# Expert weights in 4 KB rows: two experts a tile, two tiles a step, a longer ring, and an earlier overflow branch

## The chip, the cores and the metric

The kernel runs on one core of one Trainium2 chip. Its time is what the device needs for one execution, in microseconds (us). Of three runs of the kernel before, the median is 1256.03 us (1255.78 to 1259.5). The profile is of one further execution.

## What is computed

256 tokens of width 1024 go through two transformer blocks, all in float32. The first block ends in a mixture of experts: each token is sent to two of 32 experts, and every expert's weights are read, used or not. The part that matters here:

```
def hier_moe(v, w_grp, b_grp, w_exp, b_exp, w_gate, w_up, w_down):
    ...                                   # group and expert of each token, weight of each
    for e in range(MOE_N_EXPERTS):        # 32
        hdn = jax.nn.silu(vt @ w_gate[e]) * (vt @ w_up[e])          # 1024 -> 512, twice
        y = y + (combine[:, e:e + 1].astype(hdn.dtype) * hdn) @ w_down[e]   # 512 -> 1024
    return y.reshape(bsz, seq, d).astype(v.dtype)
```

Each expert has three matrices of 2 MB (512 x 1024 float32), so the experts' weights are 192 MB in all, counted in units of 1,048,576 bytes. The second block works on the same 256 tokens and on 256 context tokens. The context tokens' half does not depend on the first block.

## The kernel before

The program has four stages: the first block's mixer, the experts (`experts`), and the two layers of the second block (`x0`, `x1`). While the experts run, a second stream (`side`: `ctx0`, then `ctx1`) does the context tokens' half of the second block. `drive` takes instructions from the streams by planned costs (`yield`), and so fixes the order of TensorE (PE) when the program is built. What is planned to take how long (`DMA_TILE` for one tile's load, `DMA_MB` for a side tile's) decides how much side work stands between two products of the experts.

The experts are taken four at a time, in eight groups `q`. For each expert up to 32 tokens are collected (`slots`: a product with a selection matrix `SY` makes `xg`, the collected tokens with the model dimension on the partitions, in eight blocks of 128). The four experts of a group stand side by side in 32 columns of the array each, so four products of 128x32 by 128x512 run together.

A weight tile holds 1 MB: 128 rows of one matrix of all four experts, in 512 columns, so 4 x 2 KB on each partition. A group has 24: eight of `w_gate`, eight of `w_up`, eight of `w_down` (four row blocks for each half of the 1024 columns), 192 in all. Tiles 1 to 9 of the stage are read ahead, five into memory that is used later (`early`: kB, kB, vB, kA, kTc) and four into the ring `we` of `WE` = 4 buffers. From then on a tile's load waits until PE has done with the tile four before it. All of these loads are issued by SyncE (SP), in program order; an instruction of SP that waits holds back all loads behind it.

The side stream has its own weight tiles (`wst`), three buffers of the pool `ws`. Most are 1024 rows by 256 columns, so 8 x 1 KB on each partition. `side_next` asks for the next tile when it hands out the last one that is loaded.

If an expert is chosen by more than 32 tokens, the tokens above 32 go through a slow loop (`overflow`). `fullest` counts, every engine then reads the count (`TENSOR_LOAD` on PE, SP and the others) and branches. With these inputs the branch isn't taken. It stands at the start of group 1; SP's `TENSOR_LOAD` there waits for all DMA counters, and so for every load that was issued.

`h` is the residual stream. `hs` is a copy of it, made by GpSimd (POOL), from which the slots of groups 1 to 7 are collected, while `h` is added to.

Of the kernel before, what the change touches and what calls it, by code (L numbers as in the profile page):

```python
# [8 lines left out]
F32 = mybir.dt.float32  # L9
# [9 lines left out]
D = 1024  # L19
KD = 8  # L20
NEG = -1e30
EPS = 1e-6
CH = 2304
# [9 lines left out]
DMA_LAT = 1000  # L33
DMA_TILE = 2580
DMA_MB = 2600
AHEAD_S = 1
# [141 lines left out]
class Feed:  # L178
# [92 lines left out]
class Net:  # L271
# [94 lines left out]
    def ws_tile(self):  # L366
        return self.ws.tile([128, CH], F32, name="wst", tag="wst", bufs=WS)

# [665 lines left out]
    def mixer_out(self):  # L1034
# [7 lines left out]
        self.pre.append(next(self.tiles))  # L1042
        self.load_ctx(self.vc)
        wr = self.t(A, [128, KD, 36], "gqk")
        nc.gpsimd.dma_start(wr[:, :, 0:4], I["w_grp"][0].rearrange("(k p) n -> p k n", p=128))
# [81 lines left out]
    def route(self):  # L1127
# [72 lines left out]
    def overflow(self):  # L1200
# [3 lines left out]
        with tc.If(most > 32):  # L1204
            co = self.t(self.B, [128, 2, 32], "over")
            self.ts(co, self.rk, 32.5, op0=OP.is_ge)
            self.tt(co, co, self.C.rearrange("p t g e -> p t (g e)"), OP.mult)
            vT, w, hT = self.kTc, self.vc.rearrange("p t (a n) -> p (t a) n", a=2), self.row.rearrange("p (k n) -> p k n", k=4)
            for i in range(2):
                self.ts(self.vc[:, i], self.hs[:, i], self.y0[:, i:i + 1])  # L1210
            g = self.vcol("g_ffn", 0, 8)
            for k2 in range(4):
                b = self.transposes([(256 * j + 128 * i, self.vc[:, i, (2 * k2 + j) * 128:(2 * k2 + j + 1) * 128])
                                     for j in range(2) for i in range(2)], self.pt, "t", 2)
                self.tt(vT[:, 2 * k2:2 * k2 + 2], b.rearrange("p (k t) -> p k t", k=2),
                        g[:, 2 * k2:2 * k2 + 2, None].to_broadcast([128, 2, 256]), OP.mult)
            sc = self.dram.tile([32, 128, 2], F32, name="cover")
            for i in range(2):
                nc.sync.dma_start(sc.rearrange("e p t -> p t e")[:, i], co[:, i])
            with tc.For_i(0, 32, 1) as e:  # L1220
                cw = self.t(self.B, [128, 2], "cwe")
                nc.sync.dma_start(cw, sc[bass.ds(e, 1)].rearrange("a p t -> p (a t)"))

                def load(ap):
                    nc.sync.dma_start(w, ap.rearrange("a (k p) n -> p (a k) n", p=128))
                    return w
                gu = []
                for n, tag in (("w_gate", "g"), ("w_up", "d")):
                    bs = [self.bank(self.pe, tag, 2) for _ in range(2)]
                    for hf in range(2):  # L1230
                        v = load(I[n][0][bass.ds(e, 1), 512 * hf:512 * hf + 512])
# [12 lines left out]
                for hf in range(2):  # L1244
                    v = load(I["w_down"][0][bass.ds(e, 1), :, 512 * hf:512 * hf + 512])
                    for i in range(2):
# [4 lines left out]
                        self.stt(o, b, cw[:, i:i + 1], o, OP.mult, OP.add)  # L1251

    def slots(self, q):

# [15 lines left out]
        self.slot[q] = xg, (ST, w)  # L1270
        g = self.vcol("g_ffn", 0, 8)
        src = self.hs if q else self.h
        for k4 in range(2):
            b = self.bank(pt, "t", 2)
            for k in range(4):
                for i in range(2):
                    kk = 4 * k4 + k
                    nc.tensor.matmul(b[:, 128 * k:128 * k + 128], src[:, i, 128 * kk:128 * kk + 128], Sy[:, i],
                                     start=i == 0, stop=i == 1)
# [12 lines left out]

    def early(self):

        P = self.Q0
        b = self.t(self.Qa, [128, 2, 2048], "kB")
        yield b[:, 0]
        yield b[:, 1]
        yield self.t(P, [128, 2048], "vB")
        yield self.t(self.Qa, [128, 2048], "kA")  # L1300
        yield self.t(self.P2, [128, 2048], "kTc")

    def expert_tiles(self):

        I, early = self.I, self.early()
        for q in range(8):
            es = slice(4 * q, 4 * q + 4)
            aps = [I[n][0][es, 128 * k:128 * k + 128, :] for n in ("w_gate", "w_up") for k in range(KD)]
            aps += [I["w_down"][0][es, 128 * k:128 * k + 128, 512 * hf:512 * hf + 512] for hf in range(2) for k in range(4)]
            if not q:  # L1310
                aps = aps[WE:WE + EARLY] + aps[:WE] + aps[WE + EARLY:]
            for ap in aps:
                v = next(early, None)
                if v is None:
                    v = self.we.tile([128, 2048], F32, name="we", tag="we", bufs=WE)
                v = v.rearrange("p (e n) -> p e n", e=4)
                self.nc.sync.dma_start(v, ap.rearrange("e p n -> p e n"))
                yield v

    def expert_tile(self):  # L1320

        n = len(self.used)
        if n >= EARLY + WE:
            self.loaded = max(self.loaded, self.used[n - WE] + DMA_LAT) + DMA_TILE
# [3 lines left out]
        return v, late  # L1328

    def experts(self):  # L1330
# [4 lines left out]
        yield (-2, self.slots(0))  # L1335
        for q in range(8):
            if q == 1:
                self.overflow()
                self.gf = self.bcast_row(self.row, self.I["g_final"])
# [3 lines left out]
            for _ in range(2):  # L1343
                b = self.bank(self.pe, "g", 2)
                for k in range(KD):
                    if k == 4:
                        yield from self.wait("slot%d1" % q)
                    v, late = self.expert_tile()
# [5 lines left out]
                    if not q and WE + EARLY == KD * len(bs) + k + 1:  # L1354
                        self.keep()
                        self.done.add("keep")
                if not q and not bs:
                    self.fullest()
                    yield 400
# [14 lines left out]
            yield (450, 600)  # L1374
            ds = [self.bank(self.pe, "d", 2) for _ in range(2)]
            for hf in range(2):
                for k in range(4):
                    v, late = self.expert_tile()
# [418 lines left out]
    def ctx1(self):  # L1797
# [7 lines left out]
        for q in range(8):  # L1805
            wk = self.side_next()
            if q == 7:

                self.done.add("c6")
                yield from self.wait("experts")  # L1810
            b = self.bank(ps, "s", 2)
            if q < 4:
# [15 lines left out]
    def keep(self):  # L1828
# [7 lines left out]
        self.kA = self.t(self.Qa, [128, 4, 512], "kA", dt=F32R)  # L1836
        self.kTc = self.t(self.P2, [128, KD, 256], "kTc")
        self.gm = self.t(self.P2, [128, KD], "gm")
# [644 lines left out]
```

## Time and profile before

| | |
|---|---|
| median of three runs | 1256.03 us |
| the profiled execution | 1260.11 us |
| its span | 1258.0 us, 20010 instructions |
| PE busy | 1119.0 us, 89% |
| DVE, ACT, POOL busy | 564.2, 454.1, 191.8 us |
| read from HBM | 331.58 MB |

The span is cut into 40 slices of 31.45 us by the page. In slices 11 to 28 the DMA engines are over 90% busy and move 338 to 386 GB/s: that is the stage of the experts, from 291.04 us (the first product of an expert) to 879.28 us (the end of the last). Outside it they move 67 to 346 GB/s, and PE has most of its work in products of three parts (`gmm`).

How to read the rows further down. A windows row gives a stretch and its length, then the busy time (and count of instructions) of PE, PEld, DVE, ACT and POOL, PE's granted clock and the mean busy share of the DMA engines (both as a share of 1), and GB/s. A timeline row gives start, length, engine, line, operation, how many, and in brackets the idle time before it and what ended it. A busy PE is an engine that has a matmul in it, not one at its peak. PE's matmuls of float32 appear as two records for each product in the program. In the DMA view "GB/s" is given in 40 equal pieces of the window. Times "idle before" name what ended the idle time.

### The profile page before, as it was taken

The page shows a single profiled execution, that of the slowest core. Times are in us where ns is not written, and L with a number is a line of the kernel's source. Part 1 is how long each engine was busy: PE and PEld are TensorE (multiplying, and loading weights), DVE is VectorE, ACT ScalarE, POOL GpSimd, SP SyncE. Part 2 cuts the span into 40 slices and gives each one's busy share as a digit, 9 for nine tenths or more (in the row PEclk, how much of TensorE's full clock was granted, in tenths as well). Part 3 has the DMA queues.
Part 4 walks back from the last instruction along what each step waited for, and adds up shares of the span by engine and source line. Part 5 has one row for each costly group of instructions (what it writes and reads, how often), then busy time and mean ns, then how long its engine had stood idle before and what let it go on. Part 6 is the DMA issues. An engine that isn't in the chain of part 4 may idle for free. (4 is left out here: it accounts for less than half of the span.)

```text
span 1258.0 us, 20010 instructions
## 1 busy us (share of the span) xinstructions
PE 1119.0 (89%) x7855; PEld 778.4 (62%) x7855; DVE 564.2 (45%) x1401; ACT 454.1 (36%) x1109; POOL 191.8 (15%) x209
## 2 busy tenths in 40 slices
PE   5999999999879998788979899976999998899996
PEld 4878877785424553333336455521887787799996
DVE  5457664653121212432221211101788668777766
ACT  4534564541101101222220110101566653776663
POOL 6134012111000000000000000000311224325231
PEclk9999999988989999989999989977999999999999
DMA  7897579956999999999999999999445247365331
GB/s 252 283 305 251 189 208 323 346 187 237 363 338 375 378 379 382 386 373 357 363 354 378 382 379 378 376 386 362 135 133 157 67 107 169 118 163 130 101 119 67
DMA packets 228634, 337.63 MB, mean 268 GB/s; under 512 B 20021, under 2 KB 113274, under 8 KB 228538
## 3 DMA queue, kind: packets, MB, share of 16 engines
q1 hardware_dynamic: 227050, 333.78, 77.8%
q0 software_dynamic: 1072, 2.45, 0.8%
q8 instruction: 63, 1.03, 0.4%
q14 instruction: 33, 0.27, 0.1%
q10 hardware_dynamic: 416, 0.10, 0.1%
HBM read 331.58 MB, written 4.73 MB: 267 GB/s over the span
## 5 line engine op out<-in xcount | busy, mean ns | idle before, releaser
L318 ACT ACTIVATE whi<-wst 128x512 fp32r<-128x512 f32 (+4 forms) x240 | 149.1, 628 | 108.6 <-PE m L315 99.0
L1351 PE MATMUL g<-we,xg 128*32 128x512 f32 x984 | 145.6, 659 | 40.9 <-DMA we<-in_w_gate_dram 22.1
L218 DVE TENSOR_TENSOR wlo<-wst,whi 128x512 fp32r<-128x512 f32 (+4 forms) x180 | 138.2, 775 | 84.3 <-ACT whi L318 83.3
L218 POOL TENSOR_TENSOR wlo<-wst,whi 128x512 fp32r<-128x512 f32 (+4 forms) x60 | 80.5, 1343 | 495.9 <-ACT whi L318 420.8
L315 PE MATMUL m<-whi,uhi 128*128 128x256 f32 (+2 forms) x368 | 109.8, 298 | 2.6 <-ACT uhi L318 1.9
L315 PE MATMUL m<-wlo,uhi 128*128 128x256 f32 (+2 forms) x368 | 105.8, 288 | 2.7 <-POOL wlo L218 2.7
L315 PE MATMUL m<-whi,ulo 128*128 128x256 f32 (+2 forms) x368 | 105.7, 287 | 0.0
L315 PE MATMUL s<-cuT,wst 128*128 128x256 f32 (+1 forms) x368 | 90.6, 392 | 4.4 <-SPq L1204 4.4
L1381 PE MATMUL d<-we,hT 128*32 128x512 f32 x512 | 71.6, 639 | 25.3 <-DMA we<-in_w_down_dram 24.3
L315 PEld LDWEIGHTS s<-cuT,wst 128*128 128x128 f32 (+1 forms) x368 | 63.7, 183 | 44.8 <-issue 34.0
L1351 PEld LDWEIGHTS g<-we,xg 128*32 128x32 f32 x984 | 21.6, 112 | 100.4 <-DMA we<-in_w_up_dram 42.0
L315 PEld LDWEIGHTS m<-whi,uhi 128*128 128x128 f32 x368 | 71.4, 194 | 12.9 <-issue 5.8
L315 PE MATMUL m<-xhi,whi 128*128 128x256 f32 x256 | 75.6, 295 | 0.0
L315 PEld LDWEIGHTS m<-wlo,uhi 128*128 128x128 f32 x368 | 71.6, 194 | 2.9 <-POOL wlo L218 2.9
L315 PE MATMUL m<-xhi,wlo 128*128 128x256 f32 x256 | 72.3, 283 | 0.0
L315 PE MATMUL m<-xlo,whi 128*128 128x256 f32 x256 | 72.3, 282 | 0.0
L315 PEld LDWEIGHTS m<-whi,ulo 128*128 128x128 f32 x368 | 71.4, 194 | 0.3 <-POOL ulo L504 0.3
L315 PEld LDWEIGHTS s<-wst,cuT 128*128 128x128 f32 x256 | 43.7, 194 | 22.2 <-issue 17.6
L315 PE MATMUL s<-wst,cuT 128*128 128x256 f32 (+1 forms) x256 | 57.3, 369 | 0.0
L315 PEld LDWEIGHTS m<-xhi,whi 128*128 128x128 f32 x256 | 48.8, 191 | 2.7 <-issue 2.5
L315 PEld LDWEIGHTS m<-xlo,whi 128*128 128x128 f32 x256 | 48.9, 191 | 0.7 <-issue 0.5
L315 PEld LDWEIGHTS m<-xhi,wlo 128*128 128x128 f32 x256 | 48.8, 191 | 0.0
(592 smaller groups left out, 2183.2 us busy)
## 6 DMA issues: line engine op xcount, KB each, us to landing
we<-in_w_down_dram SPq DMA_DIRECT2D x64, 1024.0 KB
we<-in_w_up_dram SPq DMA_DIRECT2D x63, 1024.0 KB
we<-in_w_gate_dram SPq DMA_DIRECT2D x60, 1024.0 KB
we<-in_ada_w_dram SPq DMA_DIRECT2D x24, 1024.0 KB
wst<-in_c_in_w_dram SPq DMA_DIRECT2D x24, 1024.0 KB
wst<-in_w_in_dram SPq DMA_DIRECT2D x17, 1024.0 KB
wst<-in_ab_in_w_dram SPq DMA_DIRECT2D x16, 1024.0 KB
wst<-in_ab_out_w_dram SPq DMA_DIRECT2D x8, 1024.0 KB
```

Source lines behind the costliest of these rows:

```text
L218: (net.nc.gpsimd if pool else net.nc.vector).tensor_tensor(b, src, a, OP.subtract)
L315: mm(out, l, r, start=first and i == 0, stop=last and i == len(ps) - 1, skip_group_check=True)
L318: return self.nc.scalar.activation(out, in_, f, **kw)
L1351: nc.tensor.matmul(b[32 * e:32 * e + 32, :], xg[:, k, 32 * e:32 * e + 32], v[:, e], start=k == 0, stop=k == KD - 1)
L1381: nc.tensor.matmul(ds[hf][32 * e:32 * e + 32, :], hT[:, k, 32 * e:32 * e + 32], v[:, e], start=k == 0, stop=k == 3)
```

## The change

1. A tile now holds two experts instead of four, with rows of 4 KB. For `w_gate` and `w_up` a partition holds two consecutive rows of the matrix (rows 2p and 2p+1 of a block of 256: `(p r) n -> p (r n)`); for `w_down` it holds a whole row of 1024. Two tiles, one for each pair of experts, belong to a step (`expert_pair`), which makes eight products of each. Only the last group's `w_down` keeps the old tiles.
2. So that row pairs match, the collected tokens come in another order of the model dimension: `hs` is written in that order, group 0 reads `h` with a step of two elements (`pairs`), and `gp` holds `g_ffn` in that order (a small DMA of POOL).
3. The ring is four `we` buffers, one buffer `w3` taken from the three of the pool `ws`, and `kTc`; when the context tokens have been transposed out of `vc`, that joins it. `ctx1` takes `kTc` and `vc` out again. So six buffers, then seven, then six and five. Ten tiles are read ahead, in place of nine, and an eleventh goes into `vc` before the first product; of side tiles two are read ahead, in place of three.
4. `fullest` and `overflow` stand before the first product of group 0. The slow loop uses buffers of the side stream, and its loads read row pairs.
5. `DMA_TILE` goes from 2580 to 2500, `DMA_MB` from 2600 to 2700.

```
-DMA_TILE = 2580
-DMA_MB = 2600
+DMA_TILE = 2500
+DMA_MB = 2700
...
-            v = self.net.ws_tile()[:, :kd * n].rearrange("p (k n) -> p k n", k=kd)
+            v = (self.net.ws_tile() if self.loads % WS else self.net.w3_tile())[:, :kd * n].rearrange("p (k n) -> p k n", k=kd)
...
-        return self.ws.tile([128, CH], F32, name="wst", tag="wst", bufs=WS)
+        return self.ws.tile([128, CH], F32, name="wst", tag="wst", bufs=WS - 1)
+
+    def w3_tile(self):
+        return self.ws.tile([128, CH], F32, name="w3", tag="w3")
...
-        self.side_q = [next(self.sides) for _ in range(WS)]
-        self.pre += [next(self.tiles) for _ in range(EARLY + WE - 7)]
+        self.side_q = [next(self.sides) for _ in range(WS - 1)]
+        self.pre += [next(self.tiles) for _ in range(EARLY + WE - 6)]
...
-            nc.gpsimd.tensor_copy(self.hs[:, i], self.h[:, i])
+            nc.gpsimd.tensor_copy(self.hs[:, i].rearrange("p (j r c) -> p j r c", j=4, r=2), self.pairs(self.h[:, i]))
...
+    def pairs(self, row):
+
+        return row.rearrange("p (j c r) -> p j r c", j=4, r=2)
...
+            if not q and not k4:
+                self.fullest()
+                yield 400
...
-    def early(self):
+    def room(self):
 
         P = self.Q0
+        yield self.t(self.P2, [128, 2048], "kTc")
         b = self.t(self.Qa, [128, 2, 2048], "kB")
         yield b[:, 0]
         yield b[:, 1]
         yield self.t(P, [128, 2048], "vB")
         yield self.t(self.Qa, [128, 2048], "kA")
-        yield self.t(self.P2, [128, 2048], "kTc")
+        self.ring = ["we"] * WE + ["w3", "kTc"]
+        n = 0
+        while True:
+            if n == WE + 1:
+
+                self.ring.append(self.ring.pop(0))
+            n += 1
+            s = self.ring.pop(0)
+            self.ring.append(s)
+            if s == "we":
+                yield self.we.tile([128, 2048], F32, name="we", tag="we", bufs=WE)
+            elif s == "w3":
+                yield self.w3_tile()[:, :2048]
+            else:
+                yield self.t(self.P2, [128, 2048], s)
...
-            es = slice(4 * q, 4 * q + 4)
-            aps = [I[n][0][es, 128 * k:128 * k + 128, :] for n in ("w_gate", "w_up") for k in range(KD)]
-            aps += [I["w_down"][0][es, 128 * k:128 * k + 128, 512 * hf:512 * hf + 512] for hf in range(2) for k in range(4)]
+            es = [slice(4 * q + 2 * x, 4 * q + 2 * x + 2) for x in range(2)]
+            aps = [I[n][0][s, 256 * j:256 * j + 256, :].rearrange("e (p r) n -> p e (r n)", r=2)
+                   for n in ("w_gate", "w_up") for j in range(4) for s in es]
+            if q < 7:
+                aps += [I["w_down"][0][s, 128 * k:128 * k + 128, :].rearrange("e p n -> p e n") for k in range(4) for s in es]
...
+            if q == 0:
+                yield from self.wait("slot01")
+                self.overflow()
             if q == 1:
-                self.overflow()
                 self.gf = self.bcast_row(self.row, self.I["g_final"])
...
+                    v, late = self.expert_pair()
                     yield (0, late)
-                    for e in range(4):
-                        nc.tensor.matmul(b[32 * e:32 * e + 32, :], xg[:, k, 32 * e:32 * e + 32], v[:, e],
-                                         start=k == 0, stop=k == KD - 1)
-                    yield 1100
...
+                    for r in range(2):
+                        for e in range(4):
+                            nc.tensor.matmul(b[32 * e:32 * e + 32, :], xg[:, 2 * j + r, 32 * e:32 * e + 32],
+                                             v[e // 2][:, e % 2, 512 * r:512 * r + 512],
+                                             start=j == 0 and r == 0, stop=j == 3 and r == 1)
+                        yield 1000
...
+        self.ring.append("vc")
...
+            if q in (0, 4):
+                n = "vc" if q else "kTc"
+                self.ring.remove(n)
```

On PE the start of the stage reads as follows, first in the program before. `t<-SY,h` collects the tokens of group 0, `t<-M,tab` counts them (two rows of 128x32), `g<-...,xg` are the experts' products, `s<-wst,cuT` is side work.

```order
L315 MATMUL s<-wst,cuT 128x256 x2
L1278 MATMUL t<-SY,h 128x128 x8
L1351 MATMUL g<-we,xg 32x512 x4
L1278 MATMUL t<-SY,h 128x128 x8
L1351 MATMUL g<-we,xg 32x512 x4
L1286 MATMUL t<-tab,SW 128x128 x2
L1351 MATMUL g<-we,xg 32x512 x8
L1351 MATMUL g<-kB,xg 32x512 x8
```

There the first product stands behind the first half of the tokens alone, and the count comes later (it stands behind tile `kA`). The same place of PE in the changed program:

```order
L315 MATMUL s<-wst,cuT 128x256 x2
L1295 MATMUL t<-SY,h 128x128 x8
L315 MATMUL s<-wst,cuT 128x256 x2
L1201 MATMUL t<-M_3390,tab 128x32 x2
L1295 MATMUL t<-SY,h 128x128 x8
L1210 TENSOR_LOAD cnti
L1211 COMPARE_AND_BRANCH
```

Both halves of the tokens, the count and the branch now stand before the first product. (The rows between the branch and the first `g<-we,xg` are the slow loop, which is skipped.)

On SP, around the branch, the program before has these rows (`w_ukv` is a side tile's matrix).

```order
L1317 DMA we<-in_w_up_dram 128x4x512 x7
L1317 DMA we<-in_w_down_dram 128x4x512 x7
L371 DMA wst<-in_b_w_ukv_dram 128x2x1024
L1317 DMA we<-in_w_down_dram 128x4x512
L1203 TENSOR_LOAD cnti
L1203 ISA x2
L1317 DMA we<-in_w_gate_dram 128x4x512 x2
L1204 COMPARE_AND_BRANCH
```

The count is read behind all 24 tiles of group 0. In the changed program SP's branch stands here, behind the tiles that are read ahead:

```order
L374 DMA wst<-in_ab_in_w_dram 128x8x256
L1354 DMA we<-in_w_gate_dram 128x2x1024
L1354 DMA vc<-in_w_up_dram 128x2x1024
L1210 TENSOR_LOAD cnti
L1210 ISA x2
L1211 COMPARE_AND_BRANCH
```

So the branch has moved from the end of group 0's tiles to the end of the read-ahead, whose last tile now goes into `vc`.

In the dense part of the side stream (`ab_in` is the side tiles' matrix) SP reads as follows before, with the semaphores that a load waits for. `PE_49` is PE's counter, `DMAHW..` are counters of earlier loads.

```order
L1317 DMA we<-in_w_up_dram 128x4x512 [waits DMAHW6_49,PE_49]
L371 DMA wst<-in_ab_in_w_dram 128x8x256
L1317 DMA we<-in_w_up_dram 128x4x512 [waits DMAHW7_49,PE_49]
L1317 DMA we<-in_w_up_dram 128x4x512 [waits DMAHW0_49,PE_49]
L1317 DMA we<-in_w_up_dram 128x4x512 [waits DMAHW1_49,PE_49]
L371 DMA wst<-in_ab_in_w_dram 128x8x256
```

Each expert tile waits for PE here, the side tiles do not. And in the changed program (`w_4298` is a use of `w3`):

```order
L374 DMA wst<-in_ab_in_w_dram 128x8x256 [waits DMAHW4_49,PE_49]
L1354 DMA kTc<-in_w_down_dram 128x2x1024 [waits DMAHW5_49]
L1354 DMA we<-in_w_down_dram 128x2x1024 [waits DMAHW6_49]
L374 DMA wst<-in_ab_in_w_dram 128x8x256 [waits DMAHW7_49,PE_49]
L1354 DMA we<-in_w_down_dram 128x2x1024 [waits DMAHW0_49]
L1354 DMA we<-in_w_down_dram 128x2x1024 [waits DMAHW1_49]
L1354 DMA we<-in_w_gate_dram 128x2x1024 [waits DMAHW2_49]
L1354 DMA w_4298<-in_w_gate_dram 128x2x1024 [waits DMAHW3_49]
```

Now the side tiles carry the wait for PE: 18 of the 23 side loads of the changed program's stage wait for the last product of the side tile before the one that PE is at. The expert tiles behind such a load then often need no wait of their own. Where a side load waits, two expert tiles stand between it and the last one that PE has used in 11 cases, and four in 7.

## Rows read from the trace of the kernel before

**Rows 1.** Windows: the experts' stage; a light stretch; two stretches with much side work.

```profile
292.00:879.00 587.00, 503.17 (x2978) 244.38 (x2974) 119.45 (x276) 87.85 (x224) 6.17 (x6) 0.94 1.03 370
496.00:540.00 44.00, 32.45 (x242) 14.12 (x245) 17.94 (x54) 11.87 (x40) 0.00 (x0) 1.00 1.05 386
372.00:492.00 120.00, 112.33 (x664) 62.49 (x662) 21.00 (x37) 17.32 (x38) 1.05 (x2) 0.99 1.05 378
672.00:812.00 140.00, 129.82 (x728) 71.91 (x726) 25.36 (x56) 15.84 (x33) 0.00 (x0) 0.96 1.05 379
```

**Rows 2.** PE's waits, 292 to 879 us: line, releaser: us in total, times, longest.

```profile
PE d L1381 <- DMA we<-in_w_down_dram: 24.3, 25, 2.0
PE g L1351 <- DMA we<-in_w_gate_dram: 22.1, 19, 2.3
PE g L1351 <- DMA we<-in_w_up_dram: 18.0, 22, 1.6
```

**Rows 3.** Timeline of PE and ACT, end of the experts' stage.

```profile
844.11 1.94 PE L1351 MATMUL g<-we,xg 128*32 128x512 f32 x8 [0.78 <-DMA we<-in_w_up_dram]
...
849.52 1.94 PE L1351 MATMUL g<-we,xg 128*32 128x512 f32 x8 [0.78 <-DMA we<-in_w_up_dram]
...
877.34 1.94 PE L1381 MATMUL d<-we,hT 128*32 128x512 f32 x8 [1.67 <-DMA we<-in_w_down_dram]
...
880.99 0.69 ACT L318 ACTIVATE whi<-wst 128x576 fp32r<-128x576 f32 x1 [0.96 <-DMA wst<-in_ab_in_w_dram]
```

**Rows 4.** Windows: inside one load with 4 KB rows, inside one with 1 KB.

```profile
656.00:658.00 2.00, 2.00 (x10) 0.72 (x3) 0.00 (x0) 0.00 (x0) 0.00 (x0) 0.50 1.05 413
659.00:662.00 3.00, 3.00 (x17) 2.94 (x16) 0.82 (x2) 0.60 (x1) 0.00 (x0) 0.56 1.08 353
```

**Rows 5.** Timeline of SP: issue of that load with 4 KB rows.

```profile
648.98 0.37 SPq L1563 DMA_DIRECT2D cuT<-in_ctx_dram  x1
```

**Rows 6.** Timeline, start of the experts' stage, in order of time.

```profile
278.18 2.02 POOL L1133 COPY hs<-h 128x1024 f32<-128x1024 f32 x2 [13.10 <-DVE lg L324]
281.57 2.03 PE L434 MATMUL s<-tab,vc 128*128 128x128 f32 x8 [1.61 <-ACT cuT L318]
...
287.12 3.13 PE L1278 MATMUL t<-SY,h 128*128 128x128 f32 x16
291.04 1.06 PE L1351 MATMUL g<-we,xg 128*32 128x512 f32 x8 [0.78 <-DVE xg L321]
292.16 5.57 SPq L1317 DMA_DIRECT2D we<-in_w_up_dram  x4
294.12 0.69 DVE L321 TENSOR_TENSOR xg<-t,VT 128x512 f32<-128x512 f32 x1 [3.14 <-PE t L1278]
...
300.67 0.63 PE L1194 MATMUL t<-M,tab 128*128 128x32 f32 x4
...
303.08 1.99 PE L315 MATMUL s<-wst,cuT 128*128 128x256 f32 x8
...
306.00 2.05 PE L1278 MATMUL t<-SY,hs 128*128 128x128 f32 x16
```

**Rows 7.** Timeline of DVE, PE and SP at the branch.

```profile
346.61 0.41 DVE L328 TENSOR_SCALAR ccq<-ccq,rly 128x384 f32<-128x384 f32 x1
347.82 1.46 PE L315 MATMUL s<-cuT,wst 128*32 128x256 f32 x3 [4.37 <-SPq L1204]
347.92 4.46 SPq L1317 DMA_DIRECT2D we<-in_w_gate_dram  x3
```

**Rows 8.** DMA view, 340 to 355 us in 40 pieces of 0.375 us.

```profile
GB/s 366 393 371 410 366 404 377 382 399 371 404 371 377 339 235 126 82 44 38 5 0 0 44 33 49 191 317 377 399 371 410 410 344 328 224 235 246 273 306 382
```

**Rows 9.** DMA view, 622 to 640 us.

```profile
DMA packets 2598, 5.18 MB, mean 288 GB/s; under 512 B 78, under 2 KB 78, under 8 KB 2596
```

**Rows 10.** Timeline of PE before and after the side work of that dip.

```profile
620.86 1.54 PE L1701 MATMUL s<-clT,wst 128*96 128x256 f32 x6
...
627.66 2.78 PE L1381 MATMUL d<-we,hT 128*32 128x512 f32 x24
```

More of the change, by code (lines that the diff above doesn't have):

```diff
@@ L1222, in overflow, with load @@
                 nc.sync.dma_start(cw, sc[bass.ds(e, 1)].rearrange("a p t -> p (a t)"))
-                def load(ap):
-                    nc.sync.dma_start(w, ap.rearrange("a (k p) n -> p (a k) n", p=128))
+                def load(ap, pairs=False):
+                    if pairs:
+                        nc.sync.dma_start(w.rearrange("p (j r) n -> p j (r n)", r=2),
+                                          ap.rearrange("a (j p r) n -> p (a j) (r n)", p=128, r=2))
+                    else:
+                        nc.sync.dma_start(w, ap.rearrange("a (k p) n -> p (a k) n", p=128))
                     return w
@@ L1230, in overflow @@
                     for hf in range(2):
-                        v = load(I[n][0][bass.ds(e, 1), 512 * hf:512 * hf + 512])
+                        v = load(I[n][0][bass.ds(e, 1), 512 * hf:512 * hf + 512], True)
                         for k in range(4):
@@ L1300, in early @@
         yield self.t(self.Qa, [128, 2048], "kA")
-        yield self.t(self.P2, [128, 2048], "kTc")
+        self.ring = ["we"] * WE + ["w3", "kTc"]
[10 more added lines that the diff above has]
+                yield self.w3_tile()[:, :2048]
+            else:
+                yield self.t(self.P2, [128, 2048], s)
     def expert_tiles(self):
-        I, early = self.I, self.early()
+        I, room = self.I, self.room()
         for q in range(8):
-            es = slice(4 * q, 4 * q + 4)
-            aps = [I[n][0][es, 128 * k:128 * k + 128, :] for n in ("w_gate", "w_up") for k in range(KD)]
-            aps += [I["w_down"][0][es, 128 * k:128 * k + 128, 512 * hf:512 * hf + 512] for hf in range(2) for k in range(4)]
+            es = [slice(4 * q + 2 * x, 4 * q + 2 * x + 2) for x in range(2)]
[3 more added lines that the diff above has]
+                aps += [I["w_down"][0][s, 128 * k:128 * k + 128, :].rearrange("e p n -> p e n") for k in range(4) for s in es]
+            else:
+                aps += [I["w_down"][0][28:32, 128 * k:128 * k + 128, 512 * hf:512 * hf + 512].rearrange("e p n -> p e n")
+                        for hf in range(2) for k in range(4)]
             if not q:
-                aps = aps[WE:WE + EARLY] + aps[:WE] + aps[WE + EARLY:]
+                aps = aps[WE + 1:WE + 1 + EARLY] + aps[:WE + 1] + aps[WE + 1 + EARLY:]
             for ap in aps:
[L1313 to L1317, printed above, removed]
+                v = next(room).rearrange("p (e n) -> p e n", e=ap.shape[1])
+                self.nc.sync.dma_start(v, ap)
                 yield v
@@ L1322, in expert_tile @@
         n = len(self.used)
-        if n >= EARLY + WE:
-            self.loaded = max(self.loaded, self.used[n - WE] + DMA_LAT) + DMA_TILE
+        if n >= EARLY + WE + 1:
+            self.loaded = max(self.loaded, self.used[n - len(self.ring)] + DMA_LAT) + DMA_TILE
         v = self.pre.pop(0) if self.pre else next(self.tiles)
@@ L1328, in expert_tile, with expert_pair @@
         return v, late
+    def expert_pair(self):
+        a, _ = self.expert_tile()
+        b, late = self.expert_tile()
+        return (a, b), late
     def experts(self):
@@ L1344, in experts @@
                 b = self.bank(self.pe, "g", 2)
-                for k in range(KD):
-                    if k == 4:
+                for j in range(4):
+                    if j == 2:
                         yield from self.wait("slot%d1" % q)
-                    v, late = self.expert_tile()
+                    v, late = self.expert_pair()
                     yield (0, late)
-                    for e in range(4):
-                        nc.tensor.matmul(b[32 * e:32 * e + 32, :], xg[:, k, 32 * e:32 * e + 32], v[:, e],
-                                         start=k == 0, stop=k == KD - 1)
-                    yield 1100
-                    if not q and WE + EARLY == KD * len(bs) + k + 1:
+                    for r in range(2):
[4 more added lines that the diff above has]
+                        yield 1000
+                    if not q and WE + 1 + EARLY == KD * len(bs) + 2 * j + 2:
                         self.keep()
                         self.done.add("keep")
-                if not q and not bs:
-                    self.fullest()
-                    yield 400
                 if q < 7 and not bs:
@@ L1375, in experts @@
             ds = [self.bank(self.pe, "d", 2) for _ in range(2)]
+            for k in range(4 if q < 7 else 0):
+                v, late = self.expert_pair()
+                yield (0, late)
+                for hf in range(2):
+                    for e in range(4):
+                        nc.tensor.matmul(ds[hf][32 * e:32 * e + 32, :], hT[:, k, 32 * e:32 * e + 32],
+                                         v[e // 2][:, e % 2, 512 * hf:512 * hf + 512], start=k == 0, stop=k == 3)
+                    yield 1000
             for hf in range(2):
-                for k in range(4):
+                for k in range(4 if q == 7 else 0):
                     v, late = self.expert_tile()
```

27 lines of the change are left out of this document (18 added, 9 removed).

## The prediction

> **What bounds the kernel now.** I read the table of windows first. In the stage of the experts, 587 us of the span, the DMA engines are busy all the time at 370 GB/s and PE 503 us of it [rows 1]. The list of waits then says what PE lacks: 66 waits for expert weights, 24.3 + 22.1 + 18.0 = 64.4 us [rows 2]. The timeline of the stage's end shows it cleanly: each row of eight records is one tile's products, they start every (849.52 - 844.11) / 2 = 2.705 us, and each waits for its tile [rows 3], though PE needs 1.94 us for them there and 1.06 in a busier place [rows 3, 6]. One tile of 1.0486 MB in the light stretch, where nothing disturbs the loads, takes 1.0486 / 386 = 2.717 us [rows 1], which agrees with that spacing. So the stage is as long as its bytes take, plus what the queue stands empty. PE is not far behind: it is busy 112.3 of 120 us and 129.8 of 140 us in the two stretches with much side work [rows 1].
>
> The profiled execution took 1260.11 us, 4.1 more than the median of three, 1256.03. I add the terms as a difference, and take the difference off the median.
>
> **The change part by part.**
>
> Rows of 4 KB. No expert tile has them before, but one load does: the context tile, 1 MB, issued at 648.98 [rows 5], behind some three other loads, so that its start isn't waited for. While it flows, 413 GB/s; in a side tile with 1 KB rows, 353 [rows 4]; with 2 KB, 386. On each of 16 engines a row then takes 1024 x 16 / 353 = 46.4 ns, 84.9 ns, 158.7 ns. From the first two, another KB costs 38.5 ns, which puts 4 KB at 161.9 ns (405 GB/s, a tile 2.590 us); the direct reading gives 2.539 us. I take 409, 2.564 us, 0.153 less than now. 192 tiles less 11 read ahead leave 181 in the stage, and the last eight keep 2 KB: 173 x 0.153 = **-26.5**. Ends: 0, if the context tile's rate is its place in HBM rather than its rows, and 173 x 0.178 = -30.8.
>
> One rule of the Trainium skill speaks of this (DMA: Bandwidth & Descriptors, Why small descriptors are slow): a packet has a fixed overhead of about three cycles on top of one cycle per 32 bytes. By it a 1 KB row should cost 35/67 of a 2 KB row, so a side tile 2.84 us; the trace has 1.0486 / 353 = 2.97, so here a row's fixed part is larger than the rule says. By the rule alone a 4 KB tile would take 2.656 us and the term would be -10.6.
>
> Reading ahead. Two tiles more land before the stage, where the queue is idle: the last, into `vc`, may be issued once the transposes out of it end at 281.57 + 2.03 = 283.6 and takes 1.6 + 2.6 us (the 1.6 below), so it is there at 287.8, before the branch wants it. That is 2 x 2.59 = -5.2 in the stage. One side tile of 160 columns (0.655 MB, 1.9 us at 353) moves into it: together **-3.3**.
>
> The branch in the middle goes. PE stood 4.37 us there, to 347.82, DVE's last work ended at 347.02, and SP went on at 347.92 [rows 7]. What counts is the queue: over 15 us it moved 270 GB/s (the mean of the 40 pieces), not 386 [rows 8]: (386 - 270) / 386 x 15 = **-4.5**.
>
> The branch at the start comes. After the selection's 287.12 + 3.13 PE has two side products (half of the 1.99 us at 303.08, 1.0), the count (0.6) and the second half of the tokens (2.05) before the branch: 293.9. DVE's `xg` follows by 0.04 and takes 0.69; from DVE's last operation to PE's next product the old branch took 347.82 - 347.02 = 0.8. So the first product stands at 295.4 instead of 291.04. The ring's first load was issued at 292.16, one tile's product later; now a pair must be used (2.1), so 297.5: **+5.2** [rows 6]. All engines are queued behind the branch, but only this chain matters, as the queue is empty then before and after. Bounds 3 and 7. The copy `hs` with a step may take twice its 2.0 us at 278.18 and is still done before its first use at 306.00, so nothing [rows 6].
>
> A longer ring. Between 622 and 640 the queue moves 288, not 386 [rows 9], since PE was at side products from 620.86 to 627.66 [rows 10], and four tiles are 10.9 us of transfer at most, much of it already under way. Six or seven cover 15 to 18 us. (386 - 288) / 386 x 18 = **-4.6**; end 0.
>
> Side loads with two buffers. By the order of SP 18 of them now wait for PE to leave the side tile before, with everything queued behind them. In a cycle of four expert tiles and one side tile the DMA needs 4 x 2.564 + 2.97 = 13.2 us. The chain through the wait is: issue to flow 1.6 (SP at 347.92, the rate is up from 349.5 [rows 7, 8]), the side tile 2.97, the two expert tiles behind it 5.1, their pair of products 2.0, and one or two us of the side products planned between: 12.7 to 13.7, so nothing, or up to 0.5 a load; in the 7 cases with four tiles queued, nothing. As the planned order will not always be that even, I charge the upper 0.5 for each of 18: **+9**. Ends: 0, and 18 x 1.6 = +29, when the queue runs dry for the issue each time.
>
> PE in the dense stretches. Before, a cycle is 4 x 2.717 + 2.97 = 13.84 us, so 13.2 is 0.956 of it: 120 us become 114.7 against PE's 112.3, 140 become 133.8 against 129.8 [rows 1]. It fits on the average, less so piece by piece: **+2**, ends 0 and all the gain of the two stretches: 260 / 13.84 x 4 = 75 tiles x 0.153 = 11.5.
>
> End of the stage. The last expert product starts at 877.34 after its tile, and the next layer's first weights arrive behind it in the same queue, wanted at 880.99 [rows 3]; that order is as before, so what the stage gains the layers behind it get in full.
>
> Sum: -26.5 - 3.3 - 4.5 + 5.2 - 4.6 + 9 + 2 = -22.7, so 1237.4 for the profiled execution and **1233** by the median. Its own range: gains from 15 to 35, 1221 to 1241.
>
> **Rivals.**
> - PE takes over in the dense stretches, and their 75 tiles gain nothing: -22.7 + 11.5 - 2 = -13.2, **1243**. For it: 94% busy there. Against it: seven tiles of lead even out what four did not.
> - A row's fixed cost is smaller than the rows of 1 KB suggest, and 4 KB go at 395 GB/s, half-way from 386 to 405: 2.655 us, 173 x 0.062 = -10.7 for -26.5, and PE then isn't in the way (0 for +2): -8.9, **1247**. For it: 413 is a window of 2 us, inside a single load. Against it: the side tile's 353. The Trainium skill's rule above comes to the same.
> - Rows don't matter: 0 for -26.5 and for +2; of the side loads' +9 half remains, as a cycle is 0.6 longer: -2.7, **1253**, no change. Against it: two sizes in one trace, 353 and 386, beside the same work.
> - Slower: the two side buffers. Without them the sum is -31.7, so from 31.7 / 18 = 1.76 us a load they eat it all. If each waiting side load leaves the queue empty for as long as one expert tile takes, 2.6 us, the place being the dense stretches, it is 46.8 - 31.7 = +15.1, **1271**. For it: SP issues in order, and only two expert tiles cover the wait. Against it: a chain of 12.7 to 13.7 us beside a cycle of 13.2.
> - More: 413 GB/s throughout and no wait at the side loads: -30.8 - 3.3 - 4.5 + 5.2 - 4.6 = -38, **1218**.
>
> **How the numbers follow.** The forecast gets 0.52, PE 0.17, the smaller row cost 0.09, no effect 0.07, slower 0.10, more 0.05. A measurement here can tell 0.3%, 3.8 us, from no change. Faster are the forecast, PE's, the smaller cost and more: 0.83; same 0.07; slower 0.10. The range reaches up past the smaller row cost and stops short of "no effect" and "slower", which hold 0.17, and down past "more": 1214 to 1252.
>
> **What would show it.** Right: in the last group's `w_up` the products' spacing falls from 2.705 to about 2.57 us; stretches of 4 KB rows alone move 400 GB/s or more; the wait of 4.4 us in the middle is gone, and one of about 1.5 stands before the first product, at 295; the queue no longer falls where the side products of 620 to 628 us stand; PE's waits for weights fall from 64 to some 40 us. SP's waits before `wst` stay short of emptying the queue. Wrong: a rate of 386 as before in the light stretches (rows don't matter); rates under 350 around each side load, with PE waiting for expert tiles behind it (two buffers); PE busy over 97% of the dense stretches (PE).

## The result and the profile after

The changed kernel takes 1238.06 us (median of 4, 1237.95 to 1239.08) against 1256.92 (median of 4, with the three of the forecast): 0.9849 of it, 95% interval 0.9831 to 0.9866. That is 19 us faster, of the 22.7 forecast (1233, range 1214 to 1252). Its profiled span is 1237.3 us, 20.7 shorter than before.

The first view is the table of windows, for the stage, a light stretch and two with much side work; it answers to [rows 1].

```profile
299.00:858.00 559.00, 492.81 (x2944) 254.66 (x2936) 115.34 (x270) 86.97 (x222) 5.61 (x5) 0.99 1.00 384
480.00:520.00 40.00, 30.19 (x208) 12.09 (x200) 17.13 (x54) 12.38 (x41) 0.00 (x0) 1.00 1.03 408
380.00:480.00 100.00, 97.27 (x548) 58.95 (x548) 16.55 (x29) 13.69 (x26) 0.00 (x0) 1.00 0.99 374
640.00:780.00 140.00, 130.67 (x729) 76.11 (x728) 21.49 (x50) 14.44 (x31) 0.00 (x0) 1.00 0.97 368
```

The light stretch goes from 386 to 408 GB/s, but the dense ones, which moved 378 and 379 before, are slower than before. So rows of 4 KB do what was forecast, and something else takes part of it back, just where the side work is dense.

PE's waits for weights are now split by buffer, since the ring's buffers have several names; the largest four, against [rows 2]:

```profile
PE g L1396 <- DMA we<-in_w_gate_dram: 9.4, 7, 2.2
PE g L1396 <- DMA we<-in_w_up_dram: 7.9, 9, 1.6
PE d L1432 <- DMA we<-in_w_down_dram: 7.1, 6, 1.8
PE d L1424 <- DMA we<-in_w_down_dram: 6.8, 7, 1.5
```

With eight smaller groups for `w`, `vc` and `kTc` they come to 41.5 us, where 64.4 stood. In the last group's `w_up` the products follow each other at the tiles' pace, as in [rows 3]:

```profile
816.87 1.05 PE L1396 MATMUL g<-we,xg 128*32 128x512 f32 x4 [0.65 <-DMA we<-in_w_up_dram]
819.42 1.91 PE L1396 MATMUL g<-we,xg 128*32 128x512 f32 x12 [1.50 <-DMA we<-in_w_up_dram]
```

The step from one tile to the next is 2.55 us (2.705 before, 2.57 forecast). The stage's start, from the timelines of PE and SP, is this, against [rows 6]:

```profile
291.41 2.13 PE L1295 MATMUL t<-SY,h 128*128 128x128 f32 x16
295.82 1.33 PE L1396 MATMUL g<-we,xg 128*32 128x512 f32 x8 [2.28 <-DVEq L1211]
299.66 2.88 SPq L1354 DMA_DIRECT2D we<-in_w_up_dram  x4
```

The first product stands at 295.82 (forecast 295.4), and the ring's first load goes at 299.66 (forecast 297.5), since the first pair of tiles is used more slowly: eight records take 1.33 us, not 1.06. PE stood for 2.28 us just before, and its granted clock is 0.71 from 297.70 to 301.50, a mean of its two levels of 1.2 and 2.4 GHz, where it was 1.00 (2.4 GHz) from 290 to 294. The last product of an expert ends at 858.15, 21 us sooner than before.

Where the queue loses, the list of SP's waits from 292 to 858 us names it first (us in total, times, longest): SP waits before a side tile's load (L374) for a side product of PE. The DMA view from 640 to 660 us, in pieces of 0.5 us, with the timelines of SP and PE shows one case:

```profile
SPq L374 <- PE s L315: 172.6, 17, 14.9
```

```profile
GB/s 418 401 410 401 401 279 287 238 0 0 0 0 25 158 276 332 385 373 377 404 408 410 401 418 418 410 410 401 410 410 418 410 410 410 401 410 410 418 410 377
```

```profile
643.34 3.72 PE L315 MATMUL s<-wst,cxa 128*128 128x256 f32 x16
645.37 0.37 SPq L374 DMA_DIRECT2D wst<-in_ab_out_w_dram  x1
645.79 0.58 SPq L1354 DMA_DIRECT2D w<-in_w_gate_dram  x1
```

SP stands before a side tile's load until PE is through with an older side tile; when it goes at 645.37, the expert tiles behind it go at once, so their buffers were free. From 642.5 the queue runs out, from 644 to 646 nothing moves, and at 648, 2.6 us after SP's issue, the rate is back at 385 GB/s. There are seven such dips at side loads (324, 408, 436, 464, 642, 715 and 759 us). Their pieces of 0.5 us under 300 GB/s together lose 17.8 us against 408 GB/s. Before, the branch and a full ring of four made the dips of [rows 8, 9].

### The profile page after: what moved, and what is told of

The parts are those of the page before. It is cut to its first block, busy times and chain, and to the rows that moved or that the text cites. A ratio compares the mean times of both kernels' runs of the same rounds, so it can differ in the third digit from the quotient of the medians.

```text
span 1237.3 us, 19978 instructions
## 1 busy us (share of the span) xinstructions
PE 1114.7 (90%) x7855; PEld 793.0 (64%) x7855; DVE 562.3 (45%) x1401; ACT 453.3 (37%) x1109; POOL 192.2 (16%) x210
## 5 line engine op out<-in xcount | busy, mean ns | idle before, releaser
L1396 PE MATMUL g<-we,xg 128*32 128x512 f32 x624 | 109.8, 613 | 19.8 <-DMA we<-in_w_gate_dram 9.4
L318 ACT ACTIVATE whi<-wst 128x512 fp32r<-128x512 f32 (+1 forms) x158 | 98.4, 629 | 74.7 <-PE m L315 69.1
L218 DVE TENSOR_TENSOR wlo<-wst,whi 128x512 fp32r<-128x512 f32 (+2 forms) x119 | 93.9, 796 | 64.2 <-ACT whi L318 63.6
L315 PE MATMUL s<-cuT,wst 128*128 128x256 f32 (+1 forms) x368 | 85.6, 385 | 0.7 <-ACT cuT L318 0.7
L315 PEld LDWEIGHTS m<-whi,uhi 128*128 128x128 f32 x368 | 71.5, 194 | 12.9 <-issue 5.8
L218 POOL TENSOR_TENSOR wlo<-wst,whi 128x512 fp32r<-128x512 f32 (+1 forms) x39 | 52.2, 1339 | 175.9 <-ACT whi L318 134.9
L218 POOL TENSOR_TENSOR wlo<-w,whi 128x512 fp32r<-128x512 f32 (+4 forms) x21 | 28.0, 1334 | 326.0 <-ACT whi L318 291.7
L318 ACT ACTIVATE whi<-w 128x512 fp32r<-128x512 f32 (+4 forms) x82 | 50.9, 628 | 34.3 <-PE m L315 29.7
L324 DVE SCALAR_TENSOR_TENSOR eo<-d,STw,eo 128x512 fp32r<-128x512 f32 x16 | 12.0, 748 | 99.8 <-ACT eo L318 99.8
L1424 PE MATMUL d<-we,hT 128*32 128x512 f32 x272 | 49.3, 600 | 7.5 <-DMA we<-in_w_down_dram 6.8
```

Source lines behind the costliest of these rows:

```text
L218: (net.nc.gpsimd if pool else net.nc.vector).tensor_tensor(b, src, a, OP.subtract)
L315: mm(out, l, r, start=first and i == 0, stop=last and i == len(ps) - 1, skip_group_check=True)
L318: return self.nc.scalar.activation(out, in_, f, **kw)
L324: return self.nc.vector.scalar_tensor_tensor(out, a, s, b, op0=op0, op1=op1, **kw)
L1396: nc.tensor.matmul(b[32 * e:32 * e + 32, :], xg[:, 2 * j + r, 32 * e:32 * e + 32], v[e // 2][:, e % 2, 512 * r:512 * r + 512], start=j == ...
L1424: nc.tensor.matmul(ds[hf][32 * e:32 * e + 32, :], hT[:, k, 32 * e:32 * e + 32], v[e // 2][:, e % 2, 512 * hf:512 * hf + 512], start=k == 0 ...
```

## The experiments

Each changes the kernel after the change unless said otherwise; each was run beside the kernel before, and the ratio is to that.

**Rows of 2 KB, all else as changed** (two_kb). The edit's main lines; `w_down` is treated alike:

```
-            aps = [I[n][0][s, 256 * j:256 * j + 256, :].rearrange("e (p r) n -> p e (r n)", r=2)
-                   for n in ("w_gate", "w_up") for j in range(4) for s in es]
+            aps = [I[n][0][es, 256 * j:256 * j + 256, :].rearrange("e (p r) n -> p e r n", r=2)[:, :, r, :]
+                   for n in ("w_gate", "w_up") for j in range(4) for r in range(2)]
...
-                                             v[e // 2][:, e % 2, 512 * r:512 * r + 512],
+                                             v[r][:, e],
```

> The changed kernel with one thing undone: a tile is again four experts in 2 KB rows (of w_gate and w_up every second row, so that the order of the tokens' dimension stays), the ring, the branch and the two tiles a step as changed. Theory (the row's size sets the rate, 408 to 386 GB/s): a tile takes 2.72 us for 2.57, so 173 tiles lose 26; as the longer tiles hide some of the waits of the side loads, 18 to 26 slower than the changed kernel's 1238, 1256 to 1264, and the light stretches fall back to 386 GB/s. Rival (rows do not matter, the ring and the branch brought the gain): 1238 within 4, and 408 GB/s stays.

1258.44 us, ratio 1.0011 (0.9993 to 1.0029). Undoing the rows alone costs 20.4 us, the whole gain. The light stretch shows why; the same 40 us moved 408 GB/s above:

```profile
480.00:520.00 40.00, 27.25 (x199) 10.95 (x201) 17.03 (x52) 12.12 (x40) 0.00 (x0) 1.00 1.05 386
```

**Rows of 4 KB, the rest as before** (rows_only): ring of four, nine tiles read ahead, three side buffers, branch in group 1, the old planned costs; but two tiles a step. Of the edit:

```
-        self.ring = ["we"] * WE + ["w3", "kTc"]
+        self.ring = ["we"] * WE
...
-            if q == 0:
-                yield from self.wait("slot01")
-                self.overflow()
             if q == 1:
+                yield from self.wait("back01")
+                self.overflow()
```

> The other half: 4 KB rows and two tiles a step, but the ring of four, nine tiles read ahead, three side buffers, the branch in group 1 (behind the adding up of group 0's results) and the planned costs as in the kernel before. Theory (rows give 26.5 alone, ring and branch together about nothing, since what the ring gains the two side buffers take): 1228 to 1236. Rival (the ring of four, freed two tiles at a time, is too short for tiles that arrive faster, so 4 KB rows need the longer ring): 1240 to 1250, with more stretches under 400 GB/s beside side products than in the changed kernel.

1260.92 us, ratio 1.0047 (1.0025 to 1.0069): a miss for both, it is even a little slower than before. The DMA view from 820 to 850 us in pieces of 0.75 us, where PE has hardly any side work (the changed kernel moves 406 from 816 to 834), and SP's timeline there:

```profile
GB/s 421 421 415 415 415 410 404 246 213 295 393 388 421 399 410 371 366 311 300 246 268 399 431 360 300 355 388 366 421 426 399 350 371 415 410 404 415 401 336 344
```

```profile
817.45 1.19 SPq L1338 DMA_DIRECT2D we<-in_w_gate_dram  x2
823.40 13.88 SPq L1338 DMA_DIRECT2D we<-in_w_up_dram  x6
```

SP issues in twos: two loads go at 817.45 and the next not before 823.40, 6 us later, while two 4 KB tiles take 5.1 us. At 825.25 the rate falls to 246, and it is back at 393 only in the piece from 827.5. The ring of four, freed two tiles at a time, has two tiles in flight while PE is at the other two. The next run tests that.

**The same with rows of 2 KB** (pairs_only), so that beside the kernel before mainly the two tiles a step are new; the edit is that of the first run, on the second.

> The run with the old ring and 4 KB rows took 1260.9 us where 1228 to 1236 was expected. This is the same kernel with 2 KB rows (four experts a tile), so that beside the kernel before only the two tiles a step are new. Theory (two tiles a step free the ring of four in pairs, so that only two tiles are in flight while PE is at the other two, and the queue runs dry): 6 to 16 slower than the kernel before, 1263 to 1272, with stretches under 380 GB/s also where PE has little to do; 4 KB rows then give 3 to 12 of it back with that ring. Rival (two tiles a step cost nothing; 4 KB rows are worth nothing while the ring is four): 1256 to 1260.

1269.82 us, ratio 1.0096 (1.0069 to 1.0123), as the theory had it: two tiles a step cost 12.9 us with a ring of four, and 4 KB rows give 8.9 of it back. Where PE has little to do, the expectation fails in one place and holds in another. At the end of the stage the queue stays full: the DMA view from 820 to 870 us has 386 GB/s with 2 KB. The light stretch from 496 to 540 us, which moved 386 in the kernel before [rows 1], moves 360, with PE busy 32 of 44 us:

```profile
DMA packets 9710, 19.30 MB, mean 386 GB/s; under 512 B 294, under 2 KB 294, under 8 KB 9709
```

```profile
496.00:540.00 44.00, 32.35 (x231) 14.91 (x229) 17.95 (x53) 12.12 (x39) 0.00 (x0) 0.96 1.01 360
```

**Three side buffers, ring one shorter** (three_side), and one expert tile fewer read ahead, one side tile more.

```
-        return self.ws.tile([128, CH], F32, name="wst", tag="wst", bufs=WS - 1)
+        return self.ws.tile([128, CH], F32, name="wst", tag="wst", bufs=WS)
...
-        self.ring = ["we"] * WE + ["w3", "kTc"]
+        self.ring = ["we"] * WE + ["kTc"]
```

> The changed kernel with three buffers for the side stream again and the ring one shorter (four we and kTc, then vc), one expert tile fewer read ahead, one side tile more. Theory (the side loads' wait for PE with two buffers empties the queue, some 9 us): 1229 to 1234, and the dips to under 100 GB/s behind SP's waits before side loads are gone. Rival (PE is what is full there, or the ring's length is worth as much): 1236 to 1242.

1222.79 us, ratio 0.9744 (0.9712 to 0.9776), 15.3 faster than the changed kernel. The third buffer is worth more than the ring's seventh. None of the seven dips is left, and SP hardly waits before side loads any more. Its wait there, and the stretch that stood still from 644 to 646:

```profile
SPq L374 <- PE s L315: 1.9, 2, 1.0
```

```profile
GB/s 410 426 393 410 393 418 401 426 410 418 410 401 393 401 371 395 354 363 340 371 389 358 387 389 404 410 410 410 434 401 410 410 401 410 401 418 418 410 410 410
```

**Side loads asked for elsewhere** (late2, late_fix, late_fix4). The buffers stay two; the place of a side load in SP's order moves, and with it the point at which `drive` counts the load's planned cost.

```
     def expert_tile(self):
         n = len(self.used)
+        if n >= self.due:
+            self.side_load()
...
-        if len(self.side_q) < AHEAD_S:
-            t = next(self.sides, None)
...
+        self.due = len(self.used) + 2
```

> The changed kernel with two side buffers as they are, but a side tile's load stands two expert tiles further back in SP's order than where the last loaded side tile is handed out. Theory (it is the place of the side loads' wait in SP's order that empties the queue; two more expert tiles are issued ahead of it): 5 to 12 faster than 1238, 1226 to 1233. Rival (what three side buffers bring, 1222.8, is the third buffer itself: side tiles come too late when they are asked for later, and PE waits for them): 1238 to 1246, with PE waits for wst.

1289.87 us, ratio 1.0264 (1.0236 to 1.0292), 52 slower than the changed kernel: neither. The edit had dropped the condition that no loaded side tile is left, so from the first one on each load was asked for a tile sooner and waited for the side tile in progress. SP's wait for it grows, in the same row of the list:

```profile
SPq L374 <- PE s L315: 256.1, 20, 19.0
```

So this run lengthened the wait instead of shortening it, and the time went up with it. With the condition back (`if len(self.side_q) < AHEAD_S: self.due = len(self.used) + 2`):

> In the run before it, a side tile's load was asked for at every side tile handed out, also at the first, so from then on each load waited for the end of the side tile in progress, one tile sooner than meant: that run priced the opposite. Here, with two side buffers, a load is asked for only when none is left, and two expert tiles later than in the changed kernel. Theory (with two more expert tiles issued ahead of SP's wait the seven dips at side loads shrink): 5 to 13 faster than 1238, 1225 to 1233. Rival (the two tiles only shift the wait, since the ring is then as full and the side tile comes that much later): 1235 to 1245.

1221.99 us, ratio 0.9717 (0.9685 to 0.9749), 16 faster than the changed kernel, with its two buffers and its ring. SP still waits at 16 side loads, but with more tiles on their way; the whole stage then runs at 398 GB/s (second row), and the dense stretch from 380 to 480 us, 374 above, at 397 (third row):

```profile
SPq L374 <- PE s L315: 97.3, 16, 9.2
```

```profile
299.00:840.00 541.00, 486.31 (x2930) 254.28 (x2923) 116.77 (x271) 87.78 (x223) 5.62 (x5) 0.97 1.03 398
380.00:480.00 100.00, 96.82 (x551) 57.69 (x553) 18.51 (x35) 12.48 (x27) 0.00 (x0) 0.97 1.04 397
```

PE is busy 96.82 of these 100 us, as it was before the fix (97.27). So a PE that busy did not hold the queue at 374; the waits at side loads did.

Four expert tiles later in place of two:

> As the version that asks for a side tile two expert tiles later (1222.0), but four later. Theory (with two the queue is full at every side load already, 398 GB/s over the stage; nothing is left to gain there): 1220 to 1225. Rival (four later the side tile lands after PE wants it, and PE waits for wst): 1228 to 1240.

1223.35 us, ratio 0.9731 (0.9698 to 0.9764): nothing more to gain, nothing lost.

**Rows of 2 KB with three side buffers** (three_two_kb); the edit is that of the first run, on the version with three side buffers.

> The version with three side buffers (1222.8) with 2 KB rows: four experts a tile, everything else as there. Theory (where no side load empties the queue, 4 KB rows are worth their full transfer time, 26.5): 1246 to 1251. Rival (they are worth no more than the 20 of the changed kernel, since PE fills what the queue leaves): 1238 to 1244.

1245.28 us, ratio 0.9916 (0.9883 to 0.9950). Undoing the rows costs 22.5 here, between the two expectations.

**Without the branch** (no_branch, three_no_branch): the call of `overflow` is left out.

> The changed kernel without the overflow branch; it leaves out the slow loop for experts with more than 32 tokens, which these inputs do not take. The count stays. Theory (before the first product the branch costs only what stands between the second half of the tokens and the first product, 2.3 us of PE's wait, of which the multiplication of the tokens stays): 1.5 to 3 us faster than 1238, 1235 to 1237. Rival (the branch holds SP and so the first loads by the whole delay of the first load, 299.7 for 292.2): 1230 to 1232.

1238.25 us, ratio 0.9850 (0.9819 to 0.9881): no gain, a miss for both. The ring's first load goes at 293.65, 6 us earlier (2.3 of that is there already at the tokens' second half, 289.14 for 291.41). How long the lead lasts can be read from ACT's rows for `hT`, one in each group: first those of groups 0 and 5 of the changed kernel, then without the branch.

```profile
320.91 0.60 ACT L318 ACTIVATE hT<-t 128x512 f32<-128x512 f32 x1 [0.77 <-PE t L437]
...
684.90 0.60 ACT L318 ACTIVATE hT<-t 128x512 f32<-128x512 f32 x1 [17.56 <-PE t L437]
```

```profile
315.04 0.60 ACT L318 ACTIVATE hT<-t 128x512 f32<-128x512 f32 x1 [0.77 <-PE t L437]
...
684.65 0.60 ACT L318 ACTIVATE hT<-t 128x512 f32<-128x512 f32 x1 [17.19 <-PE t L437]
```

A lead of 5.9 us in group 0 is 0.25 in group 5. I took it that the dips had used it up, and tested that with three side buffers, where there are none at side loads:

> The version with three side buffers without the overflow branch; it leaves out the slow loop for experts with more than 32 tokens, which these inputs do not take. In the changed kernel the same edit brought the first loads 5 us forward and the end not at all. Theory (there the head start was lost again at the side loads, whose times PE sets; without their dips it lasts): 4 to 6 faster than 1222.8, 1217 to 1219. Rival (the dense stretches are PE's, and the head start is lost there in any case): 1221 to 1224.

1220.47 us, ratio 0.9719 (0.9686 to 0.9753), 2.3 faster than with the branch; the intervals of the two overlap, so between the two expectations, and the time does not decide. The traces say more: with three side buffers the lead lasts. It is 3.9 us at `hT` of group 0 (323.84 with the branch, 319.98 without) and 5.1 at that of group 7, first with the branch, then without:

```profile
821.76 0.60 ACT L318 ACTIVATE hT<-t 128x512 f32<-128x512 f32 x1 [22.10 <-PE t L437]
```

```profile
816.68 0.60 ACT L318 ACTIVATE hT<-t 128x512 f32<-128x512 f32 x1 [21.75 <-PE t L437]
```

So the lead goes only where side loads wait. With two buffers it falls in two steps, from 5.9 to 3.0 us between groups 0 and 1 and from 2.8 to 0.25 between groups 4 and 5, and in both spans the rate is under 300 GB/s at a side load for longer than with the branch: 4 us against 1 between 333 and 341, 7.5 against 5 between 639 and 648. What part of the two steps is the queue's, and what part PE's, is not separated.

**The branch in group 1 again** (branch_back).

```
-            if q == 0:
-                yield from self.wait("slot01")
-                self.overflow()
             if q == 1:
+                yield from self.wait("back01")
+                self.overflow()
```

> The changed kernel with the overflow branch in group 1 again (behind the adding up of group 0's results, in the buffers of the changed version; the count stays early). Theory (the forecast's terms: the queue loses 4.5 in the middle again, and the later start is mostly the tokens' second half, not the branch, as its removal gave nothing): 1240 to 1244. Rival (with six or seven tiles in the ring the branch has more to wait for: all of them must land first, and PE stands while the queue drains): 1246 to 1255, with a PE wait of 8 us or more at the branch.

1241.67 us, ratio 0.9885 (0.9862 to 0.9909), as the theory had it, 3.6 slower; its interval and the changed kernel's just touch. PE's wait there is as long as in the kernel before (4.37, [rows 7]), with a longer ring:

```profile
348.35 3.75 PE L315 MATMUL s<-wst,cuT 128*128 128x128 f32 x16 [4.53 <-PEq L1211]
```

**The planned costs of before** (old_plan): `DMA_TILE = 2580`, `DMA_MB = 2600`.

> The changed kernel with the planned costs of the kernel before (2580 for a tile, 2600 for a side MB). Theory (the planned costs place some side products otherwise, but the queue and PE's work stay): within 4 of 1238. Rival (the places of the side products decide how long SP stands before a side load, so a plan by other costs shifts the empty stretches): 1243 or more, or 1233 or less.

1241.35 us, ratio 0.9878 (0.9849 to 0.9906): within 4, and the intervals overlap.

## Why the prediction was right, and where its terms were off

The direction and the likeliest case held, with 19 of 22.7 us. The terms one by one:

- **Rows of 4 KB, -26.5, with +2 for PE.** The mechanism is right: 408 GB/s (taken 409), a step of 2.55 us (2.57), and undone alone it costs 20.4 with the changed ring and 22.5 where no side load empties the queue. A sum by 386 and 408 would be 173 x (2.717 - 2.570) = 25.4, so 3 to 5 are not collected; where they stay isn't shown. The rule of the Trainium skill that was weighed (DMA: Bandwidth & Descriptors, Why small descriptors are slow) gave an estimate of 10.6; the trace disagrees, the light stretch moves 408, and by the rule 4 KB tiles of 2.656 us would have moved 395.
- **Two tiles a step.** This the forecast put at nothing, without a reason: it looked at what the ring holds, not at how it is freed. With the ring of four it costs 12.9 (the run of pairs alone), more than the longer ring's term of -4.6. The longer ring therefore does more than fill a dip. With pairs and three side buffers in both versions, the longer ring and what came with it (the reading ahead, the branch, the plan) are worth 1269.82 - 1245.28 = 24.5 with rows of 2 KB, and 1260.92 - 1222.79 = 38.1 with rows of 4 KB; of this the branch is 3.6 by its own run, and the ring alone had none. The parts do not add up singly: rows are worth 8.9 with the old ring and 20.4 with the new.
- **Two side buffers, +9.** The rival "slower" had the right mechanism, the forecast its right sign, and the size lies between: 15.3 and 16.1 by the two runs that take the wait's cover back, 17.8 summed over the dips. It is not 0.5 for each of 18 waits but 1.4 to 3.5 at seven of them. The chain of 12.7 to 13.7 us was right for an even plan; the plan isn't even. In the dip at 642 us PE has 20 records of side products, a pair of tiles and 16 more such records in one go, 637.08 to 647.06, and SP's load is released only within the last of these.
- **The branch.** Moving it from the middle to the start brings 3.6, and as it costs nothing measurable at the start (1238.25 without it), that is what the middle cost (forecast 4.5). In front of the first product it moves that to 295.82, as forecast. The step that fails is that the queue's later start, +5.2 (297.5 - 292.16 is 5.3; measured 7.5), is paid in full at the end: a lead of 5.9 us does not last beyond group 5, though with three side buffers one of 3.9 lasts to the end of the stage. The run without the branch leaves the count and the second half of the tokens in front, so their share of the +5.2 has no run of its own.
- **Reading ahead, the end of the stage.** The next layer's first weights are used at 860.62, 20.4 us sooner than 880.99 [rows 3]: what the stage gained went through to the end. Reading ahead had no run of its own.

Of the signs of being wrong two came as well, and the prediction had tied them to rivals. Rates far under 350 GB/s stood at side loads, so that rival was real in part. PE was busy 97.27 of 100 us in one dense stretch, but that rival was not: without the waits at side loads the same stretch runs at 397 GB/s beside an equally busy PE.

That the sum was near is in part luck. Side loads cost some 7 more than forecast and rows brought 2 to 4 less than the 24.5 that were left after PE's +2, while the later start cost 5 less. By difference, as an estimate, the longer ring, the reading ahead and the pairs together come to -8 to -11, near the -7.9 forecast, but as a small remainder of much larger parts. The version with the later side loads, 1221.99, beats the changed kernel by 16 us, the whole of the mis-sized term as measured, and the kernel before by 35.

## What to carry to other kernels

A bigger transfer row is worth its time only if buffers come free as fast as tiles arrive: look at how many tiles are in flight when a step frees two at once, not at how many the ring holds. Where one queue issues two kinds of loads in order, the kind that waits sets the lead of the other; count the tiles issued between the event that it waits for and its place, and try to move the request later before adding buffers. And undo parts singly and together: here the whole change is worth 19 us, and its rows, with the pairs that they need, cost 4 when they come without the ring.

## What the runs showed of the hardware

Rows of 4 KB reached 408 GB/s over 40 us on one core (480 to 520 us of the changed kernel), 2 KB 386 in the same window of two_kb, and 1 KB, inside one side tile of the kernel before, 353 over 3 us [rows 4]. With 2 KB, reading every second row of a matrix (a step of 4 KB, two_kb and pairs_only) went at the same 386 as consecutive rows [rows 1]. After an empty queue the first bytes flowed within 1.1 us of SP's issue, and the rate was at 385 GB/s again after 2.6 (the dip at 642 us).
